# Attention scores with all 128 rows of TensorE in every matmul

## The chip, the cores and the metric

The kernel runs on one core of a Trainium2 chip. A core has a matrix engine (TensorE, in the profile PE, its weight loads PEld), a vector engine (VectorE, DVE), a scalar engine (ScalarE, ACT), a general engine (GpSimd, POOL) and DMA queues (SP and others). The metric is the device time of one execution in microseconds, as the median of three runs; lower is better.

## What is computed

The reference is a decoder trunk of two layers on 512 positions of width 1024, in float32. Layer 0 mixes tokens by windowed attention with sinks (8 query heads, 2 key heads of 64) beside a convolution module; layer 1 by dilated attention (8 heads of 64) beside a gated unit. A SwiGLU feed-forward part follows each mixer. The scores are what this case is about:

```python
s = jnp.einsum('bnqhgd,bnjhd->bnhgqj', qb, kk, preferred_element_type=jnp.float32) * (hd ** -0.5)
s = jnp.where(valid[None, :, None, None], s, -jnp.inf)
p = jnp.exp(s - m[..., None])
o = jnp.einsum('bnhgqj,bnjhd->bnqhgd', p.astype(v.dtype), vv, preferred_element_type=jnp.float32)
```

A head is 64 wide, so a score matmul has a contraction of 64 where TensorE has 128 rows.

## The kernel before

Nearly all products are made of float32 values split into a high part, which the matmul type `F32R` holds, and a low part, the rest. A weight product takes three matmuls: high with high, high with low, low with high (`acc3`, L200 to L202). Activations lie transposed: 128 channels on the partitions, 512 positions in the columns.

The order of PE's instructions is the program's own: `seq` is a clock in estimated time by which the weight products (`gemm0`, `gemm1`, `tok_gemm`) are interleaved with the steps of attention, which are generators that yield a cost and a waiting time. The constants of `C0` say how long after a query projection its scores come, and how long after the scores the values. The queues of the other engines are ordered by a planner when the kernel is built, from a model of its own; work marked `LATER` (the convolution taps, L470 to L478) fills their gaps.

In both mixers two heads share a tile: head b=0 in partitions 0 to 63, head b=1 in 64 to 127. Since a head needs only 64 rows, high and low parts are stacked on the two halves, so that one matmul of 128 rows gives two of the products, and a second matmul on 64 rows adds the third.

Layer 0 (`scores0`, L561). The queries of a head are stacked: `qss[b]` holds the high part in the rows of the head and the low part in the other half (L707, L708). `khh[b]` holds the high part of the keys in both halves (L687, L688), and `kl` the low part of both key heads, each in its own half (L689). For a block of 128 queries n = 1 to 3, a matmul on 128 rows (L582) gives high·high plus low·high, and one on 64 rows (L583) adds high·low, both with 256 keys in the columns. For block n=0 one float32 matmul on 64 rows with 128 keys takes the unsplit `qT` and `kT` (L580); the hardware makes it in two passes, which the profile counts as two matmuls. A step of `scores0` has two blocks of queries and both heads: n = 0 and 1 in eight instructions, then, after more of the projections, n = 2 and 3 in eight. Scores stand in PSUM banks 2 (b=0) and 3 (b=1). DVE reads them (L590, row minimum and mask), ACT takes the exponentials (L602), PE transposes the result (L406), ACT copies it (L409), PE multiplies with the values (L420), DVE normalises (L429), PE transposes back (L434). There are four such rounds, one for each query tile i.

Layer 1 (`stack`, L1085, and `scores1`, L1104). `qs` holds the high part of a head's queries in both halves, `ks` the high part of its keys in the head's half and the low part in the other (L1092 to L1096), `ql` the low part of the queries of both heads. Block n has (n+1)·128 keys: a matmul on 128 rows (L1118) and one on 64 rows (L1119) for each head, four instructions a step and four steps in a round, in four rounds. DVE reads with L1122, ACT takes exponentials with L1126.

Of the kernel before, what the change touches and what calls it, by code (L numbers as in the profile page):

```python
# [23 lines left out]
P = 128  # L24
# [109 lines left out]
def trunk_kernel(ctx: ExitStack, tc: tile.TileContext, xT, ws, cols, sinks, sgu_g, sgu_b,  # L134
# [308 lines left out]
    with ExitStack() as mx:  # L443
# [94 lines left out]
                free.extend((0, 1))  # L538
            return gemm0(free.pop(0))

        kT = mp.tile([P, S], F32, name="kT")


        khh = [mp.tile([P, S], F32R, name=f"khh{b}") for b in range(2)]
        kl = mp.tile([P, S], F32R, name="kl")
        rows = (slice(0, 64), slice(64, 128))
        Vt = mp.tile([P, NQ, P], F32, name="Vt")

        def v_tok(vT):
# [11 lines left out]
        def scores0(i):  # L561
            yield 0.0, C0["q"]
            while i >= 2 and ("V", i - 2) not in done:
                yield 0.0, 0.3
            qT, qss = qTs[i]
            Pm = mp.tile([P, 8, 2 * P], F32, name="Pm", bufs=2)
            nm = scr.tile([P, 8], F32, name="nm")
            l = scr.tile([P, 8], F32, name="l")
            for n2 in range(2):
                sb = [bank(2), bank(3)]  # L570
                for n1 in range(2):
                    n = 2 * n2 + n1
                    for b in range(2):
                        r = slice(64 * b, 64 * b + 64)
                        lo = max(n - 1, 0) * P
                        w = (n + 1) * P - lo
                        out = sb[b][:, n1 * 256 + 256 - w:n1 * 256 + 256]
                        q = slice(n * P, (n + 1) * P)
                        if n == 0:
                            T.matmul(out, qT[r, q], kT[r, lo:lo + w], start=True, stop=True)  # L580
                        else:
                            T.matmul(out, qss[b][:, q], khh[b][:, lo:lo + w], start=True, stop=False)  # L582
                            T.matmul(out, qss[b][r, q], kl[r, lo:lo + w], start=False, stop=True)  # L583
                for n1 in range(2):
                    n = 2 * n2 + n1
                    for b in range(2):
                        u = 2 * n + b
                        c0 = P if n == 0 else 0
                        hd = i + 4 * b
                        V.tensor_tensor_reduce(  # L590
                            out=Pm[:, u, c0:], in0=sb[b][:, n1 * 256 + c0:n1 * 256 + 256],
                            in1=mask0[:, c0:], scale=-0.125, scalar=nsink[:, hd:hd + 1],
                            op0=ALU.add, op1=ALU.min, accum_out=nm[:, u:u + 1])
                if n2 == 0:
                    yield 0.9, C0["S"]
            es = scr.tile([P, 8], F32, name="es")
            V.tensor_tensor(out=es.rearrange("p (n b) -> p n b", b=2),
                            in0=nm.rearrange("p (n b) -> p n b", b=2),
                            in1=sinkb[:, i:i + 5:4][:, None, :].to_broadcast([P, NQ, 2]), op=ALU.add)
            for u in range(8):  # L600
                c0 = P if u < 2 else 0
                A.activation(Pm[:, u, c0:], Pm[:, u, c0:], AF.Exp, bias=nm[:, u:u + 1], scale=-1.0,  # L602
                             accum_out=l[:, u:u + 1])
            A.activation(es, es, AF.Exp)
            rl = scr.tile([P, 8], F32, name="rl")
            V.tensor_add(rl, l, es)
            V.reciprocal(rl, rl)
            del qTs[i]
            pend[i] = Pm, rl, seq.t + 0.9 + C0["ST"]
            yield 0.9, 0.0  # L610
# [62 lines left out]
        for step in C0["steps"].split():  # L673
# [7 lines left out]
            elif kind == "k":  # L681
                ps = gemm_in(step)

                def after(ps=ps):
                    rope(ps, kT, tabs, V if "k" in C0["rope_v"] else G)
                    for b in range(2):
                        A.activation(khh[b][rows[b]], kT[rows[b]], AF.Copy)  # L687
                        A.activation(khh[b][rows[1 - b]], kT[rows[b]], AF.Copy)  # L688
                        V.tensor_tensor(out=kl[rows[b]], in0=kT[rows[b]], in1=khh[b][rows[b]], op=ALU.subtract)  # L689
            elif kind == "v":  # L690
                ps = gemm_in(step)

# [349 lines left out]
    with ExitStack() as mx:  # L1042
# [37 lines left out]

        rows = (slice(0, 64), slice(64, 128))

        def stack(qT, kT):  # L1085
            ql = mp.tile([P, S], F32R, name="ql", bufs=2)
            out = []
            for b in range(2):
                r, o = rows[b], rows[1 - b]
# [1 line left out]
                qs = mp.tile([P, S], F32R, name="st", bufs=8)  # L1091
                A.activation(qs[r], qT[r], AF.Copy)  # L1092
                A.activation(qs[o], qT[r], AF.Copy)
                V.tensor_tensor(out=ql[r], in0=qT[r], in1=qs[r], op=ALU.subtract)
                A.activation(ks[r], kT[r], AF.Copy)
                V.tensor_tensor(out=ks[o], in0=kT[r], in1=ks[r], op=ALU.subtract)  # L1096
                out.append((qs, ks))
# [6 lines left out]
        def scores1(i, qk, ql):  # L1104
# [6 lines left out]
            for n in range(NQ):  # L1111
# [2 lines left out]
                sb = [bank(2), bank(3)]  # L1114
                for b in range(2):
                    qs, ks = qk[b]
                    r = rows[b]
                    T.matmul(sb[b][:, :w], qs[:, q], ks[:, :w], start=True, stop=False)  # L1118
                    T.matmul(sb[b][:, :w], ql[r, q], ks[r, :w], start=False, stop=True)  # L1119
                for b in range(2):  # L1120
                    u = 2 * n + b
                    V.tensor_tensor_reduce(  # L1122
# [32 lines left out]
        for i in range(4):  # L1155
# [3 lines left out]
            ps = gemm1(1)  # L1159
            kT = mp.tile([P, S], F32, name="kT")  # L1160
            rope(ps, kT, tabs)
            seq.add("S1", scores1(i, *stack(qT, kT)))
            seq.add("V1", values1(i))


# [149 lines left out]
```

## Time and profile before

| | us |
|---|---|
| median of three runs | 1143.85 |
| lowest and highest | 1141.49, 1144.53 |
| the profiled execution, its own time | 1142.52 |
| its span, first to last instruction | 1140.8 |
| PE busy | 1093.2 (96%) |
| DVE busy | 704.1 (62%) |
| ACT busy | 568.5 (50%) |
| POOL busy | 244.4 (21%) |
| mean granted clock of TensorE | 0.98 |

A profile records each instruction's start and duration on its engine and what ended the wait ahead of it. Matmuls are pipelined: the duration of one overlaps the next, so what a matmul costs PE is the distance from its start to the next one's start. The operands `64*128` and `128*128` are the rows and columns of the array that a matmul uses; `64x256` is the operand that streams, 256 columns on 64 rows.

### The profile page before, as it was taken

What the parts mean: (1) busy time and instruction counts of PE and PEld (TensorE: products, weight loads), DVE (VectorE), ACT (ScalarE), POOL (GpSimd) and SP (SyncE); (2) the same over time, 40 slices, a digit from 0 to 9 for tenths busy, and PEclk for the clock granted to TensorE, in tenths of its full rate; (3) what the DMA queues carried; (4) which work ended last, traced back from release to release, by engine and by line L of the source; (5) the groups of instructions that cost most, each with busy time, mean ns of one, the idle gap of its engine ahead of it and who ended that gap; (6) DMA issues with size and microseconds to landing.
All of it is one profiled execution on the core that took longest, in us unless ns stands there. A gap on an engine that the chain in (4) does not pass through costs nothing.

```text
span 1140.8 us, 13569 instructions
## 1 busy us (share of the span) xinstructions
PE 1093.2 (96%) x5052; PEld 890.2 (78%) x5052; DVE 704.1 (62%) x1060; ACT 568.5 (50%) x920; POOL 244.4 (21%) x218
## 2 busy tenths in 40 slices
PE   6989899899999999999999999999899999999997
PEld 4867678788888888888887878787688888888785
DVE  6789875677565655664647545664865656556533
ACT  4477656664435343543546654445644353434533
POOL 5788655201101010100024200002011010101002
PEclk9989899899999999999999999999999999999999
DMA  5221102887867677621522111238878776776121
GB/s 212 74 75 48 46 19 92 214 227 190 181 185 148 184 142 208 139 47 56 167 92 67 45 38 42 88 97 219 218 188 182 185 148 185 142 209 138 29 74 74
DMA packets 42802, 145.87 MB, mean 128 GB/s; under 512 B 4848, under 2 KB 5744, under 8 KB 42736
## 3 DMA queue, kind: packets, MB, share of 16 engines
q1 hardware_dynamic: 31216, 103.06, 26.9%
q0 software_dynamic: 11520, 41.95, 21.7%
q8 instruction: 39, 0.64, 0.2%
q14 instruction: 27, 0.22, 0.1%
HBM read 142.89 MB, written 2.10 MB: 127 GB/s over the span
## 4 chain that ended last, share of the span: by engine, by line
PE 80%; DVE 7%; ACT 4%; issue 3%; POOL 3%; DMA 2%; SPq 0%; POOLq 0%; ACTq 0%; DVEq 0%
PE bank L200 11%; PE bank L892 11%; PE bank L895 11%; PE bank L894 11%; PE bank L201 10%; PE bank L202 10%; PE bank L261 2%; PE bank L420 2%; PE bank L263 2%; PE bank L262 2%; DMA raw<-in_ws 2%; PE bank L907 1%; PE bank L406 1%; DVE w2l L150 1%; PE bank L1119 1%
## 5 line engine op out<-in xcount | busy, mean ns | idle before, releaser
L150 DVE TENSOR_TENSOR w2l<-raw,w2h 128x1024 fp32r<-128x1024 f32 x140 | 171.5, 1226 | 203.4 <-ACT w2h L868 203.0
L868 ACT ACTIVATE w2h<-raw 128x1024 fp32r<-128x1024 f32 x140 | 148.0, 1059 | 207.3 <-PE bank L895 159.8
L173 ACT ACTIVATE w_hi<-raw 128x512 fp32r<-128x512 f32 x204 | 128.1, 629 | 199.1 <-PE bank L201 146.2
L858 POOL DMA_DIRECT2D raw<-in_ws x80 | 69.4, 879 | 558.9 <-DVE w2l L150 226.2
L150 DVE TENSOR_TENSOR w_lo<-raw,w_hi 128x512 fp32r<-128x512 f32 x161 | 115.2, 716 | 64.1 <-ACT w_hi L173 64.1
L892 PE MATMUL bank<-w2h,s 128*128 128x512 f32 x320 | 126.1, 394 | 3.6 <-ACT s L811 1.9
L894 PE MATMUL bank<-w2l,s 128*128 128x512 f32 x320 | 125.5, 392 | 1.8 <-DVE w2l L150 1.8
L895 PE MATMUL bank<-w2h,s 128*128 128x512 f32 x320 | 125.5, 392 | 0.0
L200 PE MATMUL bank<-xh,w_hi 128*128 128x512 f32 x272 | 115.4, 424 | 9.9 <-ACT xh L312 9.9
L201 PE MATMUL bank<-xl,w_hi 128*128 128x512 f32 x272 | 112.0, 412 | 2.8 <-DVE xl L313 2.8
L202 PE MATMUL bank<-xh,w_lo 128*128 128x512 f32 x272 | 110.9, 408 | 0.0
L200 PE MATMUL bank<-hh,w_hi 128*128 128x512 f32 x256 | 99.9, 390 | 0.0
L201 PE MATMUL bank<-hl,w_hi 128*128 128x512 f32 x256 | 99.8, 390 | 0.0
L202 PE MATMUL bank<-hh,w_lo 128*128 128x512 f32 x256 | 99.8, 390 | 0.0
L892 PE MATMUL bank<-w2h,xh 128*128 128x512 f32 x240 | 94.5, 394 | 0.0
L895 PE MATMUL bank<-w2h,xl 128*128 128x512 f32 x240 | 93.6, 390 | 0.0
L894 PE MATMUL bank<-w2l,xh 128*128 128x512 f32 x240 | 93.5, 390 | 0.0
L892 PEld LDWEIGHTS bank<-w2h,s 128*128 128x128 f32 x320 | 60.5, 189 | 16.7 <-ACT s L811 2.3
L200 PEld LDWEIGHTS bank<-xh,w_hi 128*128 128x128 f32 x272 | 54.3, 200 | 23.4 <-ACT xh L312 10.8
L894 PEld LDWEIGHTS bank<-w2l,s 128*128 128x128 f32 x320 | 60.4, 189 | 14.4 <-DVE w2l L150 2.1
L150 POOL TENSOR_TENSOR w_lo<-raw,w_hi 128x512 fp32r<-128x512 f32 x43 | 59.9, 1395 | 50.4 <-ACT w_hi L173 45.0
L895 PEld LDWEIGHTS bank<-w2h,s 128*128 128x128 f32 x320 | 60.5, 189 | 13.1 <-DVE s L150 0.4
(234 smaller groups left out, 2067.6 us busy)
## 6 DMA issues: line engine op xcount, KB each, us to landing
raw<-in_ws SPq DMA_DIRECT2D x181, 512.0 KB, 4.1
raw<-in_ws POOLq DMA_DIRECT2D x80, 512.0 KB, 5.5
h<-in_xT SPq DMA_DIRECT2D x8, 256.0 KB, 6.5
out_y<-xh SPq DMA_DIRECT2D x4, 256.0 KB, 2.0
out_y<-xl SPq DMA_DIRECT2D x4, 256.0 KB, 2.3
raw<-in_ws SPq DMA_DIRECT2D x2, 256.0 KB, 4.1
ropeC<-in_rope_c SPq DMA_DIRECT2D x2, 256.0 KB, 4.1
ropeS<-in_rope_s SPq DMA_DIRECT2D x2, 256.0 KB, 4.6
```

Of the source, the lines that this page charges most:

```text
L150: eng.tensor_tensor(out=out, in0=a, in1=b, op=ALU.subtract)
L173: A.activation(hi, src, AF.Copy)
L200: T.matmul(ps, hi, xh, start=start, stop=False)
L201: T.matmul(ps, hi, xl, start=False, stop=False)
L202: T.matmul(ps, lo, xh, start=False, stop=stop)
L261: T.matmul(ps[t], xh[:, c], hi, start=(k == 0), stop=False)
L262: T.matmul(ps[t], xh[:, c], lo, start=False, stop=False)
L858: nc.gpsimd.dma_start(t, ws[base + 8 * (g - 1) + 2 * BLOCK_OF[more] + q], accum_op=ALU.add)
L868: A.activation(hi, src, AF.Copy)
L892: T.matmul(ps[t], xh[:, c], wh[:, w], start=(start and j == 0), stop=False, skip_group_check=True)
L894: T.matmul(ps[t], xh[:, c], wl[:, w], start=False, stop=False, skip_group_check=True)
L895: T.matmul(ps[t], xl[:, c], wh[:, w], start=False, stop=(j == 3), skip_group_check=True)
```

## The change

Low parts get tiles of their own for each head, whose other half is zero, and every score matmul then takes all 128 rows. In layer 0 `kl` becomes two tiles; the half that holds no low part is filled with zeros once, by ACT from zeroed padding (`cp[0]`). Block n=0 is computed from the split operands as the others are, so it has four F32R matmuls on 128 rows in place of two float32 ones on 64 (four passes). `kT` moves from a tile of its own into the scratch buffer `gb`. In layer 1 four tiles `qlow` (two rounds by two heads) take the place of the two `ql`, with one half zeroed once by ACT; four fills of 64x512. The number of score instructions, their columns and their order stay.

```diff
-        kl = mp.tile([P, S], F32R, name="kl")
+        kl = [mp.tile([P, S], F32R, name=f"kl{b}") for b in range(2)]
+        for b in range(2):
+            A.activation(kl[b][rows[1 - b]], cp[0][rows[1 - b], 0:1].to_broadcast([64, S]), AF.Copy)
...
-                        if n == 0:
-                            T.matmul(out, qT[r, q], kT[r, lo:lo + w], start=True, stop=True)
-                        else:
-                            T.matmul(out, qss[b][:, q], khh[b][:, lo:lo + w], start=True, stop=False)
-                            T.matmul(out, qss[b][r, q], kl[r, lo:lo + w], start=False, stop=True)
+                        T.matmul(out, qss[b][:, q], khh[b][:, lo:lo + w], start=True, stop=False)
+                        T.matmul(out, qss[b][:, q], kl[b][:, lo:lo + w], start=False, stop=True)
...
+                    kT = scr.tile([P, S], F32, name="gb")
...
-                        V.tensor_tensor(out=kl[rows[b]], in0=kT[rows[b]], in1=khh[b][rows[b]], op=ALU.subtract)
+                        V.tensor_tensor(out=kl[b][rows[b]], in0=kT[rows[b]], in1=khh[b][rows[b]], op=ALU.subtract)
...
+        qlow = [[mp.tile([P, S], F32R, name=f"ql{p}{b}") for b in range(2)] for p in range(2)]
+        for p in range(2):
+            for b in range(2):
+                A.activation(qlow[p][b][rows[1 - b]], mhalf[rows[1 - b], 0:1].to_broadcast([64, S]),
+                             AF.Copy, scale=0.0)
...
-                V.tensor_tensor(out=ql[r], in0=qT[r], in1=qs[r], op=ALU.subtract)
+                V.tensor_tensor(out=ql[b][r], in0=qT[r], in1=qs[r], op=ALU.subtract)
...
-                    T.matmul(sb[b][:, :w], ql[r, q], ks[r, :w], start=False, stop=True)
+                    T.matmul(sb[b][:, :w], ql[b][:, q], ks[:, :w], start=False, stop=True)
```

## Rows read from the trace of the kernel before

**Rows 1.** Page, parts 1 and 4: busy time of each engine; shares of the chain.

```profile
PE 1093.2 (96%) x5052; PEld 890.2 (78%) x5052; DVE 704.1 (62%) x1060; ACT 568.5 (50%) x920; POOL 244.4 (21%) x218
...
PE 80%; DVE 7%; ACT 4%; issue 3%; POOL 3%; DMA 2%; SPq 0%; POOLq 0%; ACTq 0%; DVEq 0%
```

**Rows 2.** Windows of both mixers: stretch, length, busy by engine, clock, DMA share, GB/s.

```profile
36.00:177.00 141.00, 129.68 (x617) 102.51 (x616) 118.50 (x230) 91.20 (x191) 106.20 (x80) 0.93 0.16 53
...
583.00:705.00 122.00, 118.24 (x612) 94.10 (x611) 67.03 (x149) 68.15 (x143) 24.80 (x17) 0.99 0.17 53
```

**Rows 3.** Timeline of PE, layer 0, blocks 2 and 3: start, length, instruction.

```profile
93.67 0.39 PE L202 MATMUL bank<-xh,w_lo 128*128 128x512 f32 x1
93.89 0.28 PE L582 MATMUL bank<-khh,qs 128*128 128x256 f32 x1
94.10 0.38 PE L583 MATMUL bank<-kl,qs 64*128 64x256 f32 x1
94.41 0.38 PE L582 MATMUL bank<-khh,qs 128*128 128x256 f32 x1
...
96.28 0.50 PE L200 MATMUL bank<-xh,w_hi 128*128 128x512 f32 x1
96.62 0.40 PE L201 MATMUL bank<-xl,w_hi 128*128 128x512 f32 x1
```

**Rows 4.** Timeline of PE, layer 0, blocks 0 and 1 of the second round.

```profile
87.95 0.40 PE L202 MATMUL bank<-xh,w_lo 128*128 128x512 f32 x1
88.28 0.49 PE L580 MATMUL bank<-kT,qT 64*128 64x128 f32 x4
...
89.95 0.66 PE L434 MATMUL bank<-ident,on 128*128 128x128 f32 x4
```

**Rows 5.** Timeline of PE, layer 1, steps 0, 2, 3: first matmul, one behind them.

```profile
624.22 0.31 PE L1118 MATMUL bank<-st 128*128 128x128 f32 x1
...
625.22 1.11 PE L420 MATMUL bank<-Vt,pts 128*128 128x64 f32 x8
...
633.71 0.34 PE L1118 MATMUL bank<-st 128*128 128x384 f32 x1
...
635.08 0.66 PE L434 MATMUL bank<-ident,on 128*128 128x128 f32 x4
...
637.65 0.40 PE L1118 MATMUL bank<-st 128*128 128x512 f32 x1
...
639.61 0.39 PE L201 MATMUL bank<-xl,w_hi 128*128 128x512 f32 x1
```

**Rows 6.** Timeline of PE, eight transposes in a row, merged into one line.

```profile
620.77 1.04 PE L406 MATMUL bank<-ident,Pm 128*128 128x128 f32 x8
```

**Rows 7.** Timeline of PE, end of the first step of layer 0.

```profile
71.06 0.58 PE L583 MATMUL bank<-kl,qs 64*128 64x256 f32 x1 [2.22 <-DVE kl L689]
71.57 0.80 PE L200 MATMUL bank<-xh,w_hi 128*128 128x512 f32 x1
```

**Rows 8.** Timeline of DVE, layer 0; in brackets its idle time and what ended it.

```profile
79.19 0.48 DVE L590 CUSTOM_DVE_ANT_0 Pm<-bank,mask,nsink 128x256 f32<-128x256 f32 x1 [0.98 <-PE bank L583]
...
101.40 0.69 DVE L389 TENSOR_TENSOR ra<-bank,ropeC 128x512 f32<-128x512 f32 x1 [1.19 <-PE bank L202]
...
129.91 0.48 DVE L590 CUSTOM_DVE_ANT_0 Pm<-bank,mask,nsink 128x256 f32<-128x256 f32 x1 [2.41 <-PE bank L583]
```

**Rows 9.** Windows, as rows 2, of three shorter stretches.

```profile
101.40:124.60 23.20, 19.79 (x103) 15.53 (x102) 22.98 (x40) 14.78 (x28) 19.58 (x14) 0.92 0.15 46
70.00:77.00 7.00, 5.94 (x15) 4.61 (x16) 5.27 (x13) 4.42 (x11) 7.00 (x6) 0.55 0.22 75
585.00:590.00 5.00, 5.00 (x23) 4.13 (x22) 2.63 (x5) 1.27 (x2) 2.36 (x2) 1.00 0.23 83
```

**Rows 10.** Single lines of code: count, duration in ns (least/median/most), first and last start.

```profile
L1093 ACT ACTIVATE st<-qT x8: 628/630/634, 591.3 to 656.0; 64x512 fp32r<-64x512 f32 x8
...
L478 DVE SCALAR_TENSOR_TENSOR bank<-cp,cc,bank x72: 699/754/757, 39.4 to 166.6; 128x512 f32<-128x512 f32 x72
```

More of the change, by code (lines that the diff above doesn't have):

```diff
@@ L539, in gemm_in @@
             return gemm0(free.pop(0))
-        kT = mp.tile([P, S], F32, name="kT")
         khh = [mp.tile([P, S], F32R, name=f"khh{b}") for b in range(2)]
-        kl = mp.tile([P, S], F32R, name="kl")
+        kl = [mp.tile([P, S], F32R, name=f"kl{b}") for b in range(2)]
         rows = (slice(0, 64), slice(64, 128))
+        for b in range(2):
+            A.activation(kl[b][rows[1 - b]], cp[0][rows[1 - b], 0:1].to_broadcast([64, S]), AF.Copy)
         Vt = mp.tile([P, NQ, P], F32, name="Vt")
@@ L564, in scores0 @@
                 yield 0.0, 0.3
-            qT, qss = qTs[i]
+            qss = qTs[i][1]
             Pm = mp.tile([P, 8, 2 * P], F32, name="Pm", bufs=2)
@@ L573, in scores0 @@
                     for b in range(2):
-                        r = slice(64 * b, 64 * b + 64)
                         lo = max(n - 1, 0) * P
@@ L1083, in trunk_kernel, with stack @@
         rows = (slice(0, 64), slice(64, 128))
-        def stack(qT, kT):
-            ql = mp.tile([P, S], F32R, name="ql", bufs=2)
+        qlow = [[mp.tile([P, S], F32R, name=f"ql{p}{b}") for b in range(2)] for p in range(2)]
[3 more added lines that the diff above has]
+                             AF.Copy, scale=0.0)
+        def stack(i, qT, kT):
+            ql = qlow[i % 2]
             out = []
@@ L1116, in scores1 @@
                     qs, ks = qk[b]
-                    r = rows[b]
                     T.matmul(sb[b][:, :w], qs[:, q], ks[:, :w], start=True, stop=False)
-                    T.matmul(sb[b][:, :w], ql[r, q], ks[r, :w], start=False, stop=True)
+                    T.matmul(sb[b][:, :w], ql[b][:, q], ks[:, :w], start=False, stop=True)
                 for b in range(2):
@@ L1161, in trunk_kernel @@
             rope(ps, kT, tabs)
-            seq.add("S1", scores1(i, *stack(qT, kT)))
+            seq.add("S1", scores1(i, *stack(i, qT, kT)))
             seq.add("V1", values1(i))
```

## The prediction

> **What bounds the kernel.** The page comes first: PE is busy 96% of the span, no other engine over 62%, and the chain that ended last lies on PE for 80% [rows 1]. So time taken out of PE's stream counts, unless another engine holds PE at that place. The windows of the two mixers say where that may be: in layer 1 (583 to 705 us) PE is busy 118.2 of 122.0 us, DVE and ACT little more than half; in layer 0 (36 to 177) PE is busy 129.7 of 141.0, DVE 118.5, POOL 106.2, and the clock is 0.93 [rows 2]. There part of a gain can end in a wait. The timeline of PE is read next, by distances between starts, and last the timeline of DVE, for the places where it waits for PE.
>
> **What a score matmul costs now.** In a plain run of weight products a matmul of 512 columns comes 0.22 us after the one before (93.67 to 93.89). In a score step a matmul of half as many columns takes longer: the first, on 128 rows, is followed after 0.21, and from the second on every change between 64 and 128 rows comes 0.31 apart [rows 3]. Same engine, same type, fewer columns: what differs is the number of rows from one instruction to the next. Transposes, all on 128 rows with 128 columns, follow one another at (1.04-0.27)/7 = 0.11, where 0.27 is the length of one alone as the last of the eight [rows 6].
>
> **What it will cost.** No row has 128-row matmuls of 256 columns in a row. Two rows bound it: 0.11 (128 columns) below and 0.22 to 0.23 (512) above. The plain run gives 0.227/512 = 0.44 ns a column, so 256 columns stream in 0.114; that is nearest to the transposes' 0.11, so I take 0.12. By the same rate 384 columns take 0.17, 512 take 0.227, and 128 the 0.11 of the transposes. Both bounds stay for the range.
>
> **Layer 0, the sum on PE.** Blocks 2 and 3: from 93.89 to the second matmul behind the step, 96.62, is 2.73; less 0.23 for that L200 itself, 2.50. Eight matmuls at 0.12 make 0.96. Saved 1.54, four times: 6.2. Blocks 0 and 1: 87.95 to 89.95 is 2.00, less 0.23 for L202, 1.77 [rows 4]. Block 0 changes from four passes of float32 to four matmuls of 128 columns, 4 x 0.11, and block 1 takes 4 x 0.12: 0.92. Saved 0.85, three times: 2.5. The fourth of these steps, the first of the kernel, loses: today block 0 and most of block 1 are through when the last low part of the keys comes at 71.06, and one matmul is left, with L200 0.51 behind [rows 7]. After the change block 0 needs that low part as well, so the second head's low product and four matmuls of block 1 queue behind the wait: five, in a stretch where the clock is low [rows 9], so twice 0.11 to 0.12 each, about 1.1 in place of 0.51. I put down -0.5; the readers of these scores on DVE (L590) start later by about as much, and DVE has idle time behind them to take that up (5.27 of 7 us busy from 70 to 77) [rows 9]. Together 6.2+2.5-0.5 = 8.2.
>
> **How much of it arrives.** DVE's list is in order and nearly full here, so it can move forward only where it waits for PE today. Ahead of 101.4 these waits are 0.98, 0.16, 1.00 and 1.19; from 101.4 to 124.6 it works 22.98 of 23.20 us; behind that they are 1.43, 2.41, 0.97, 0.61 and 0.82 up to the last score step (three of the nine stand in [rows 8], the full stretch in [rows 9]). Walking down: L590 needs the first six of eight matmuls, so it comes 0.95 earlier, less the 0.5 lost, at 79; PE itself is held to that by the exponentials at 84, and by L429 at 90. At 101.4 PE has gained 2.6 and DVE, with 2.8 of waits and this gain at hand, also 2.6. The full stretch carries 2.6 through. Then the waits are long enough to follow PE: 5.0 at 135, 6.2 at 155. So 6.2 of 8.2 arrive; the rest ends in longer waits of PE for DVE and ACT. POOL has waits of its own before and behind the full stretch and is not tighter than DVE.
>
> **Layer 1.** Step 0: 624.22 to 625.22 is 1.00, becomes 4 x 0.11 = 0.44, saves 0.56. Step 1 is half of the eight matmuls of rows 3, 1.25 becoming 0.48: about 0.75. Step 2: 633.71 to 635.08 is 1.37, becomes 4 x 0.17 = 0.68: 0.69. Step 3: 637.65 to 639.61 less 0.23 is 1.73, becomes 4 x 0.227 = 0.91: 0.82 [rows 5]. One round 2.8, four rounds 11.3; the very first step waits for DVE between its two heads, so I count 0.4 there in place of 0.56: 11.1. PE has almost no waits here and DVE and ACT are half idle, so nearly all arrives: 11.0.
>
> **The small parts.** A zero fill costs as a copy of 64x512 does, 0.63 us on ACT [rows 10]. The four of layer 1 (2.5 us) come before the first rope, where ACT is busy 1.27 of 5 us [rows 9], the two of layer 0 (1.3 us) just behind the first weight products, and ACT is busy 91 of 141 us from there on [rows 2]: nothing on the path, and up to 1.3 and 2.5 us once if they land in front of a copy that PE awaits. `kT` in `gb` shares two buffers with the convolution gate; its life ends with the subtraction at 71, and nothing that I can place waits for it: zero, with one DVE wait of under 1 us as the upper end. The subtraction itself, its size and its number do not change. No DMA is added and none moved. What follows the mixers (norm sums, first weights of the feed-forward part) hangs on the mixers' end and moves with it.
>
> **The clock.** Three stretches in layer 0 as that of 70 to 77 run near the lower of the two levels (1.2 in place of 2.4 GHz; granted 0.55 in that window, after PE had waited 2.2 us at 71.06) [rows 7, 9]; each costs 7 x 0.45 = 3.2 us, and three of them make the 0.07 x 141 = 9.9 us that the window lacks [rows 2]. They follow waits of PE, and these waits stay or grow a little. I leave their number as it is, and count one stretch more or less, 3.2 us, into the range.
>
> **Sum.** 6.2 + 11.0 = 17.2. The profiled execution would go from 1142.5 to 1125.3; the median lies 1.3 above that execution, so 1143.85 - 17.2 = 1126.7, rounded to 1127.
>
> **Rivals.** (a) *The load lies open.* The first 128-row score matmul of a step, 256 columns, is followed after 0.21, which is 0.10 over its streaming [rows 3]; this could be a weight load that waits for the matmul before it, and might remain when all rows are alike. Then the steps cost columns plus 0.10: 0.15, 0.21, 0.26, 0.32. Layer 0 saves 4 x 0.82 + 3 x 0.33 - 0.7 = 3.6, of which 2.7 arrive, layer 1 0.40 x 4 + 0.41 x 4 + 0.33 x 4 + 0.45 x 4 = 6.4, with 0.2 off for the first step 6.2: 1135. Against it: transposes with all 128 rows and only 0.05 us of streaming follow at 0.11, and 512 columns at 0.22, not 0.32. The Trainium skill states a rule of this kind, in "TensorE: Matmul & The Clock Gate", Part 3 (Packing small matmuls — row/col tiling): a weight load overlaps a matmul in flight only when the two use different row groups. By that rule the change would take away the cover that 64 rows beside 128 might give, and rival (a) or worse would follow; rows 6 speak against it.
> (b) *DVE keeps all of layer 0.* If the planner's new order or the full stretch swallows what PE gains there, layer 1 alone is left: 1143.85 - 11 = 1133. For it: DVE 118.5 of 141 us; against it: nine waits for PE.
> (c) *Slower, by the order of the queues.* The planner builds the lists of DVE, ACT and POOL anew, from changed times and with six more ACT instructions. A convolution tap placed ahead of a score reader, L429 or a subtraction puts 0.75 us into PE's way [rows 10]. From 17.2/0.75 = 23 such taps of the 72 on, the gain is gone; with 30, 1149. For it: PE already waits for these lists; against it: the taps have the lowest priority.
> (d) *The change does not do what it says.* If the 0.31 came from two products of different operands into one bank and not from the rows, nothing is saved: 1143 to 1145. Against it: L200 to L202 change both operands at every matmul and follow at 0.22.
>
> **How the numbers follow.** My forecast has 0.68, (a) 0.12, (b) 0.10, (c) 0.05, (d) 0.05. The forecast's own range is 1120 to 1133: downward with all of layer 0's 8.2 arriving (2.0), one low-clock stretch less (3.2) and the runs' own spread (1.5); upward with one stretch more and a fill in PE's way (3.2 and 2.5). To hold eight in ten it must reach to (b) and (a), with the spread above (a): 1120 to 1137. A measurement of this kernel can tell a change of about 0.3%, 3.4 us, from none. Faster by more: the forecast, (a) and (b), less 0.02 for small parts gone wrong, 0.88. Within: (d) and a part of (c), 0.06. Slower: 0.06.
>
> **What would show it.** Right: score matmuls of 256 columns 0.11 to 0.13 apart, of 512 at 0.22 to 0.23; steps of blocks 2 and 3 near 1.0 us; the weight product behind a step no longer later than in a plain run; DVE's waits for PE of rows 8 gone or shrunk, PE's waits for DVE's L429 still there; in layer 0 about 6 us, in layer 1 about 11 us less from first to last score step. Wrong: 0.2 between score matmuls (rival a); steps short and the mixers as long as before (b); taps ahead of score readers (c). The prediction fails most easily if a low-clock stretch comes or goes, or where the lists of DVE in layer 0 are laid anew.

## The result, and the profile after

The kernel after takes 1123.7 us (median of four runs, 1120.3 to 1124.0) against 1142.7 of the kernel before in the same comparison: a ratio of 0.9836, 95% interval 0.9806 to 0.9866. Two further comparisons of the same two kernels gave 0.9885 (0.9848 to 0.9922; 1125.3 against 1137.9) and 0.9881 (0.9861 to 0.9902; 1124.35 against 1136.5). The gain is thus 12 to 19 us; 17 had been forecast, and 1127 us with a range from 1120 to 1137. The profiled execution took 1123.48 us, with a span of 1121.8. One execution of e2_layer1, a kernel told of below, took 2158.8 us, nearly twice as long as its others, and is left out of its median.

The page's busy times and the shares of the chain, as in [rows 1]:

```profile
PE 1073.6 (96%) x5052; PEld 888.4 (79%) x5052; DVE 701.2 (63%) x1060; ACT 571.7 (51%) x926; POOL 244.7 (22%) x218
...
PE 77%; DVE 8%; ACT 4%; issue 4%; POOL 4%; DMA 2%; POOLq 0%; SPq 0%; ACTq 0%; DVEq 0%
```

PE has as many instructions as before and is busy 19.6 us less; no other engine's busy time changed by more than 3.2 us. PE's share of the chain fell from 80% to 77%; DVE, POOL and issue took up one point each: a first hint that a part of the gain ended in waits.

The timeline of PE, a step of blocks 2 and 3 in layer 0 (start, length, instruction), the counterpart of [rows 3]:

```profile
89.53 0.39 PE L202 MATMUL bank<-xh,w_lo 128*128 128x512 f32 x1
89.75 0.28 PE L580 MATMUL bank<-khh,qs 128*128 128x256 f32 x1
89.87 0.28 PE L581 MATMUL bank<-kl,qs 128*128 128x256 f32 x1
...
90.58 0.28 PE L581 MATMUL bank<-kl,qs 128*128 128x256 f32 x1
90.70 0.40 PE L200 MATMUL bank<-xh,w_hi 128*128 128x512 f32 x1
90.93 0.39 PE L201 MATMUL bank<-xl,w_hi 128*128 128x512 f32 x1
```

Starts are 0.12 us apart where they were 0.31, from the first score matmul on. The weight product behind the step comes 0.12 after the last score, and its next one 0.23 later, as in any plain run. In layer 1, step 3 (512 columns), the starts are 0.22 to 0.23 apart; in step 0 (128 columns), 0.11 to 0.14 [rows 5]:

```profile
613.30 0.31 PE L1122 MATMUL bank<-st 128*128 128x128 f32 x1
613.44 0.27 PE L1123 MATMUL bank<-st,ql 128*128 128x128 f32 x1
613.56 0.27 PE L1122 MATMUL bank<-st 128*128 128x128 f32 x1
...
625.49 0.39 PE L1122 MATMUL bank<-st 128*128 128x512 f32 x1
625.72 0.39 PE L1123 MATMUL bank<-st,ql 128*128 128x512 f32 x1
...
626.40 0.39 PE L200 MATMUL bank<-xh,w_hi 128*128 128x512 f32 x1
```

Windows over the same instructions of PE in both kernels (columns as in [rows 2]): layer 0 from the last weight products before the first score to the last score step, and layer 1 from behind its first step to its end. First the kernel before, in windows that were not shown yet, then the kernel after:

```profile
62.33:163.42 101.09, 89.87 (x436) 69.92 (x434) 83.92 (x179) 68.39 (x157) 72.92 (x55) 0.90 0.13 42
606.48:692.72 86.24, 84.72 (x444) 65.95 (x443) 46.09 (x111) 49.01 (x112) 14.36 (x10) 1.00 0.15 50
```

```profile
59.24:154.43 95.19, 82.36 (x436) 70.12 (x434) 87.41 (x185) 68.68 (x157) 73.61 (x55) 0.87 0.14 45
597.83:673.90 76.07, 73.99 (x444) 64.47 (x443) 44.38 (x111) 48.30 (x112) 14.84 (x10) 1.00 0.17 56
```

To see where the difference of these lengths sits I split PE's time in three, instruction by instruction. The distance to the next start, less the wait in the next one's brackets, is the time PE spent on its own; where the granted clock was at the lower level (0.50, 1.2 in place of 2.4 GHz), half of that is put down as lost to the clock. The same split is used for all runs below. Layer 1 is counted here from shortly before its first score step.

| us | length | waits | lost to the clock | PE's own |
|---|---|---|---|---|
| layer 0, before | 101.1 | 11.2 | 9.5 | 80.4 |
| layer 0, after | 95.2 | 12.8 | 10.8 | 71.6 |
| layer 0, after, third profile (e6_after_third, below) | 96.2 | 14.9 | 9.2 | 72.0 |
| layer 1, before | 112.2 | 3.4 | 1.7 | 107.2 |
| layer 1, after | 101.9 | 4.1 | 1.7 | 96.1 |

PE's own time falls by 8.8 and 11.1 us. Layer 1 keeps 10.3 of it, layer 0 only 5.9. Of the 2.9 us that layer 0 does not keep, 1.6 are longer waits and 1.3 the clock's; in the third profile longer waits take 3.7 of 8.4. Beside these 16.2 us stand 3.1 us that went before any score was taken: there the profile before has a stretch at the lower clock (0.51 from 25 to 32 us), and the profile after has none. Between the mixers the kernel after loses 0.5. Together 18.8 of the 19.0 us by which the two spans differ.

### The profile page after: what moved, and what is told of

It is laid out like the page before. It is cut to its first block, busy times and chain, and to the rows that moved or that the text cites. A ratio compares the mean times of both kernels' runs of the same rounds, so it can differ in the third digit from the quotient of the medians.

```text
span 1121.8 us, 13570 instructions
## 1 busy us (share of the span) xinstructions
PE 1073.6 (96%) x5052; PEld 888.4 (79%) x5052; DVE 701.2 (63%) x1060; ACT 571.7 (51%) x926; POOL 244.7 (22%) x218
## 4 chain that ended last, share of the span: by engine, by line
PE 77%; DVE 8%; ACT 4%; issue 4%; POOL 4%; DMA 2%; POOLq 0%; SPq 0%; ACTq 0%; DVEq 0%
PE bank L894 11%; PE bank L891 11%; PE bank L893 11%; PE bank L200 10%; PE bank L201 10%; PE bank L202 10%; PE bank L261 2%; PE bank L263 2%; PE bank L262 2%; PE bank L420 2%; POOL yc L474 1%; DMA raw<-in_ws 1%; PE bank L906 1%; PE bank L406 1%; DVE w2l L150 1%
## 5 line engine op out<-in xcount | busy, mean ns | idle before, releaser
L173 ACT ACTIVATE w_hi<-raw 128x512 fp32r<-128x512 f32 x204 | 128.1, 629 | 185.3 <-PE bank L201 138.8
L200 PE MATMUL bank<-xh,w_hi 128*128 128x512 f32 x272 | 113.6, 418 | 10.8 <-ACT xh L312 10.8
L201 PE MATMUL bank<-xl,w_hi 128*128 128x512 f32 x272 | 110.8, 407 | 1.9 <-DVE xl L313 1.9
L202 PE MATMUL bank<-xh,w_lo 128*128 128x512 f32 x272 | 110.2, 405 | 0.0
L200 PE MATMUL bank<-hh,w_hi 128*128 128x512 f32 x256 | 99.8, 390 | 0.0
L202 PE MATMUL bank<-hh,w_lo 128*128 128x512 f32 x256 | 99.6, 389 | 0.0
L201 PE MATMUL bank<-hl,w_hi 128*128 128x512 f32 x256 | 99.6, 389 | 0.0
L891 PEld LDWEIGHTS bank<-w2h,s 128*128 128x128 f32 x320 | 60.4, 189 | 14.9 <-ACT ga L957 1.9
L200 PEld LDWEIGHTS bank<-xh,w_hi 128*128 128x128 f32 x272 | 54.1, 199 | 22.4 <-ACT xh L312 11.7
```

Source lines behind the costliest of these rows:

```text
L173: A.activation(hi, src, AF.Copy)
L200: T.matmul(ps, hi, xh, start=start, stop=False)
L201: T.matmul(ps, hi, xl, start=False, stop=False)
L202: T.matmul(ps, lo, xh, start=False, stop=stop)
L891: T.matmul(ps[t], xh[:, c], wh[:, w], start=(start and j == 0), stop=False, skip_group_check=True)
```

## The experiments

### Each layer alone

`e1_layer0` takes the new code of layer 0 with the old layer 1, `e2_layer1` the reverse. The lines by which they differ from the kernel before are the two parts of the diff ahead of the prediction; its core in e1_layer0 is

```diff
-                        if n == 0:
-                            T.matmul(out, qT[r, q], kT[r, lo:lo + w], start=True, stop=True)
-                        else:
-                            T.matmul(out, qss[b][:, q], khh[b][:, lo:lo + w], start=True, stop=False)
-                            T.matmul(out, qss[b][r, q], kl[r, lo:lo + w], start=False, stop=True)
+                        T.matmul(out, qss[b][:, q], khh[b][:, lo:lo + w], start=True, stop=False)
+                        T.matmul(out, qss[b][:, q], kl[b][:, lo:lo + w], start=False, stop=True)
```

and in e2_layer1

```diff
-                    T.matmul(sb[b][:, :w], ql[r, q], ks[r, :w], start=False, stop=True)
+                    T.matmul(sb[b][:, :w], ql[b][:, q], ks[:, :w], start=False, stop=True)
```

> Only layer 0 has the change; layer 1 is as before. My theory: about 6 us of the gain are layer 0's (5.9 between the first score step and the end of layer 0 in the two profiles), so about 1136.5 us against 1142.7. Rival, DVE keeps layer 0's gain: 1141 to 1143. A second question is the first 36 us, ahead of any score: before ran a stretch of them at the lower clock (from about 25 to 32 us) and the changed kernel did not, 3.1 us apart. If that is chance from one execution to the next, the stretch is there in some kernels and not in others, whichever change they have; if the two zero fills at the start of ACT's queue do it, it is gone here.

> Only layer 1 has the change; layer 0 is as before. Theory: 10 to 11 us, 1132 us against 1142.7, and together with the kernel that has only layer 0's part the sum of the whole change (19). Rival, the gain of one layer hangs on the other (by the phase of the clock or the planner's order): the two parts add up to 14 or less, or to 24 or more. The first 36 us have no zero fill here: if the fills remove the stretch at the lower clock, it is there; if it is chance, it may be either.

Measured: 1134.7 us for layer 0 alone, ratio 0.9966 (0.9949 to 0.9982), a gain of 3.9 us (2.0 to 5.8); 1127.7 for layer 1 alone, 0.9898 (0.9854 to 0.9942), a gain of 11.6 (6.6 to 16.6). The window of layer 0 in e1_layer0, then that of layer 1 in e2_layer1:

```profile
60.38:155.52 95.14, 82.32 (x435) 70.12 (x434) 87.41 (x185) 68.68 (x157) 73.64 (x55) 0.87 0.13 45
```

```profile
603.85:679.97 76.12, 74.02 (x443) 64.50 (x442) 44.38 (x111) 48.29 (x112) 14.84 (x10) 1.00 0.17 56
```

The part with the new code has the length of the kernel after within 0.1 us; the other part has that of the kernel before (86.27 and 101.09). So neither layer's window hangs on the change in the other, and the gains add up within their intervals: 0.0034 and 0.0102 make 0.0136, between the 0.0115 and the 0.0164 of the whole. By time, layer 0 alone brought less than the 6 us expected of it, though its window is 6 us shorter than the one in the profile of the kernel before.

### What the change of rows costs

`e3_grouped1` is the kernel before with the order of a layer 1 step altered: both matmuls of 128 rows first, then both of 64. The same matmuls, one change of rows down and up in a step in place of two.

```diff
                 for b in range(2):
                     qs, ks = qk[b]
-                    r = rows[b]
                     T.matmul(sb[b][:, :w], qs[:, q], ks[:, :w], start=True, stop=False)
+                for b in range(2):
+                    ks = qk[b][1]
+                    r = rows[b]
                     T.matmul(sb[b][:, :w], ql[r, q], ks[r, :w], start=False, stop=True)
```

> The kernel before, with layer 1's scores reordered and nothing else: both heads' matmuls on 128 rows first, then both on 64 rows. The same instructions, half the changes of row count (two in a step in place of four). Theory, the cost sits in the change from one row count to the other: a step of 512 columns takes 1.2 us or less in place of 1.73, layer 1 gains 6 to 9 us, 1134 to 1137 us; the two 64-row matmuls lie on different halves of the array and may run side by side, which would save up to 0.2 us a step more. Rival, a matmul on 64 rows is slow in itself, wherever it stands: steps as before, 1142 to 1144 us.

`e9_one64` comes from the other side: the kernel after, with the last of the four matmuls of a layer 1 step put back on 64 rows.

```diff
-                    T.matmul(sb[b][:, :w], ql[b][:, q], ks[:, :w], start=False, stop=True)
+                    r = rows[b] if b else slice(0, P)
+                    T.matmul(sb[b][:, :w], ql[b][r, q], ks[r, :w], start=False, stop=True)
```

> The kernel after with one of the four score matmuls of each layer 1 step put back on 64 rows (the second head's low product, the last of the four); its columns and all other work stay. Theory (a price for each change of row count): the pair 128 to 64 comes about 0.2 us later than two of 128 rows, and the change back to 128 rows behind it costs up to 0.2 us again, seen on whatever matmul follows. Sixteen steps: layer 1's score region grows by 3 to 6 us. Rival (64 rows slow in themselves, in proportion to columns): the matmul on 64 rows takes twice its streaming, so 0.05 more at 128 columns and 0.23 at 512, and nothing is lost behind it: 2.3 us over sixteen steps, growing with the columns. Rival (nothing below two changes a step): no growth.

Measured: e3_grouped1 1130.25 us, ratio 0.9939 (0.9916 to 0.9962); e9_one64 1122.65 in a single run. Its total does not decide, since that execution lost less to the clock in layer 0 (5.6 us by the split above, against 10.8). Layer 1 does. The timeline of PE in e9_one64, steps 1 and 3:

```profile
593.10 0.28 PE L1124 MATMUL bank<-st,ql 128*128 128x256 f32 x1
593.22 0.28 PE L1122 MATMUL bank<-st 128*128 128x256 f32 x1
593.42 0.38 PE L1124 MATMUL bank<-st,ql 64*128 64x256 f32 x1
593.74 0.50 PE L200 MATMUL bank<-xh,w_hi 128*128 128x512 f32 x1
594.08 0.40 PE L201 MATMUL bank<-xl,w_hi 128*128 128x512 f32 x1
...
600.93 0.39 PE L1122 MATMUL bank<-st 128*128 128x512 f32 x1
601.25 0.49 PE L1124 MATMUL bank<-st,ql 64*128 64x512 f32 x1
601.67 0.50 PE L200 MATMUL bank<-xh,w_hi 128*128 128x512 f32 x1
602.01 0.39 PE L201 MATMUL bank<-xl,w_hi 128*128 128x512 f32 x1
```

Step 1: the distances are 0.20, 0.32 and 0.34 where all-128-row work has 0.12, 0.12 and 0.23; the excess is 0.08, 0.20 and 0.11. Step 3: 0.32, 0.42 and 0.34 against 0.23 each; 0.09, 0.19 and 0.11. Both make 0.39 us, with twice the columns in the second; in a step of 128 columns (from 609.35 us) the excess is 0.29. So the price belongs to the change of rows and does not grow in proportion to the columns, and it falls on the matmul of fewer rows, on the first of more, and on the one behind that. "64 rows are slow in themselves" falls: it wanted an excess that grows with the columns and nothing behind the step.

The account closes within 1 us. PE's own time in layer 1 is 96.1 in the kernel after and 102.0 in e9_one64: 5.9 us for 16 changes down and up, 0.37 each. Two for each step, as before had, would give 96.1 + 32 x 0.37 = 107.9; before has 107.2. And e3_grouped1 has one a step, like e9_one64, but 99.5. Its timeline says why it is 2.5 lower still:

```profile
615.23 0.61 PE L1117 MATMUL bank<-st 128*128 128x512 f32 x2
615.78 0.50 PE L1121 MATMUL bank<-st,ql 64*128 64x512 f32 x2
616.21 0.50 PE L200 MATMUL bank<-xh,w_hi 128*128 128x512 f32 x1
```

Two matmuls of 64 rows, one in each half of the rows, take 0.43 together up to the next start, and the single one of e9_one64 took 0.42. The second came at no cost that can be seen; by the trace it starts 3 ns behind the first. In the four sizes the matmul that it saves is worth 0.11 + 0.12 + 0.18 + 0.23, four times 0.64, 2.6 us. Grouping alone thus regained 7.4 of the 10.2 us of layer 1's window (86.2 to 78.8), without a single new tile.

### The stretch at the start

`e5_after_again` is the kernel after, with no line altered, beside the runs of each layer alone and of e3_grouped1.

> The changed kernel once more, unchanged, for the spread of its profile: 1123 to 1125 us. If the stretch at the lower clock from 25 to 32 us is chance, it can be there this time, and the score steps of 256 columns stay 0.12 apart; then some 3 us of the 19 in the two profiles are not the change's. If it is the change's, it is gone again.

Measured: 1125.3 us, the second comparison told above. Windows of the early weight products: first in this profile of the kernel after, then in its first profile.

```profile
26.50:30.00 3.50, 3.50 (x12) 2.85 (x11) 0.00 (x0) 0.00 (x0) 1.28 (x2) 0.52 0.33 103
```

```profile
7.40:31.10 23.70, 20.67 (x81) 15.34 (x82) 18.22 (x20) 12.48 (x21) 12.89 (x11) 1.00 0.58 213
```

The same kernel shows a low clock here in one execution and none in the other. Other kernels have such a stretch whichever change they contain: e1_layer0, with layer 0's zero fills, is at 0.50 from 25.2 to 28.6 us, e2_layer1, without them, from 26.1 to 29.5. The 3.1 us at the start of the profiled pair are therefore not put down to the change, nor to the zero fills, which run at 2.3 us in both profiles of the kernel after.

### Scores later, to close PE's waits

The profile after has 4.2 us of waits in the very first score step (the brackets: idle time, and what ended it), and a low clock behind it:

```profile
63.48 0.33 PE L580 MATMUL bank<-khh,qs 128*128 128x128 f32 x1 [0.67 <-ACT khh L687]
65.07 0.47 PE L581 MATMUL bank<-kl,qs 128*128 128x128 f32 x1 [1.26 <-DVE kl L688]
...
67.98 0.47 PE L581 MATMUL bank<-kl,qs 128*128 128x128 f32 x1 [2.23 <-DVE kl L688]
```

`e7_later0` puts this step later in PE's order:

```diff
-            yield 0.0, C0["q"]
+            yield 0.0, C0["q"] + (4.5 if i == 0 else 0.0)
```

`e8_later` does so in layer 1 as well, with

```diff
-            yield 0.0, C0["q1"]
+            yield 0.0, C0["q1"] + (2.2 if i == 0 else 0.0)
```

and `e6_after_third` is the kernel after, with no line altered, beside them.

> The kernel after, unchanged, beside the two kernels of this call that start the first scores later. It is the yardstick for them. Expected: 1120 to 1128 us; the wait for the keys' parts in the first score step of layer 0 (0.7, 1.3 and 2.2 us on three matmuls) is there again, since it comes from the order of the work; the number of low-clock stretches in layer 0 may differ by one (1.7 us for each 3.4 us of such a stretch), since it differed between two profiles of this same kernel.

> The kernel after, with the first round's first score step of layer 0 placed 4.5 us later in PE's order (by the constant in front of the generator), so that weight products fill the time in which PE waits for khh and kl (4.2 us of waits in the profile after). Theory: the wait is lost time on the path, and the low-clock stretch right behind it (65 to 72 us, 3.4 us lost) follows from it. Then 4 us less, and up to 7 if the low-clock stretch goes as well: 1116 to 1120. Rival: the readers on DVE start later and the wait turns up again at the exponentials or at the normalised output one step on; then 1122 to 1125. Second rival: the stretch of low clock comes elsewhere in layer 0; then the wait's 4 us alone.

> As the kernel before this in the list, and in layer 1 the first round's first score step is placed 2.2 us later too, where PE waits 2.0 us for the second head's stacked keys. Theory: 1 to 2 us less than that kernel, because layer 1 has no other tight engine. Rival: no difference, the wait moves to the next step.

Measured: 1124.35 for the kernel after, 1126.3 for e7_later0 (ratio to before 0.9911, 0.9896 to 0.9925), 1130.8 for e8_later (0.9947, 0.9931 to 0.9963). Neither later start gained anything. PE's waits in layer 0's window of e7_later0, the two largest groups by what ended them (sum, count, longest):

```profile
PE bank L406 <- ACT yn L634: 8.4, 3, 6.7
PE bank L420 <- ACT pts L409: 5.8, 2, 4.5
```

The wait for `kl` is gone and 6.7 us stand one step on, before the transposes of the weights of attention. PE starts the last score matmul of the step at 69.42 us, but DVE reads the first scores (L588) only at 73.16. Its timeline:

```profile
68.74 2.34 DVE L478 SCALAR_TENSOR_TENSOR bank<-cp,cc,bank 128x512 f32<-128x512 f32 x3
...
73.16 0.35 DVE L588 CUSTOM_DVE_ANT_0 Pm<-bank,mask,nsink 128x128 f32<-128x128 f32 x1
```

Five taps and a gate product stand ahead of the readers in DVE's list; the exponentials, and L634 behind them, follow. Waits in layer 0 are 17.4 in all against 14.9 in e6_after_third, the clock's loss is 7.3 against 9.2, and the length 96.6 against 96.2. So the first rival was right in kind, though the time lies above its range; the second held as well, as a stretch at 0.50 stands behind the new wait (79.8 to 86.6 us). e8_later took 4.5 us more than e7_later0, where its rival had no difference: PE's waits in layer 1 are 7.8 us against 4.1, since the wait for the stacked keys went but the copies of L409 now hold PE for 6.1 us in five waits, where e6_after_third has 2.5 in four.

### What holds layer 0: DVE's load, or the order?

`e10_before_halftaps` and `e11_after_halftaps` leave every second of the later convolution taps out on DVE.

```diff
-                    else:
+                    elif t % 2:
                         V.scalar_tensor_tensor(acc, src, w, acc, op0=ALU.mult, op1=ALU.add)
```

> The kernel before with every second of the convolution's later taps on DVE (L478) left out; its time is not that of the full computation. It is one of a pair: the same is left out of the kernel after. Theory (DVE's nearly full list is why not all that PE saves in layer 0 arrives): with DVE relieved by about 36 taps of 0.75 us, 27 us, PE's waits for L429 and the exponentials shrink in both kernels, and the pair differs in layer 0's score region by 8 to 9 us instead of 6. Rival (DVE is not the reason; what is missing was never saved on PE): the pair differs by the same 6. Low-clock stretches are taken out, 1.7 us for each 3.4 us of them.

> The other half of the pair: the kernel after with every second of the convolution's later taps on DVE left out; its time is not that of the full computation. Theory: 8 to 9 us less than the other kernel of the pair in layer 0's score region, low-clock stretches taken out, and 10 to 11 in layer 1, where no tap runs. Rival: 6 us in layer 0 as with all taps.

Measured: 1146.0 us for the one (five runs from 1134.1 to 1146.7) and 1121.4 for the other. The spread goes with the clock: the profiled execution of e10_before_halftaps took 1146 us, with a mean clock of 0.973, and stood at 0.50 from 143.4 to 167 us; the runs of 1134 and 1135 had 0.986. Only the split is compared. Layer 0 of both, first the kernel before with half the taps, then the kernel after:

```profile
58.59:164.73 106.14, 95.42 (x436) 74.96 (x435) 67.67 (x155) 68.78 (x156) 73.47 (x56) 0.84 0.13 40
```

```profile
58.76:151.97 93.21, 79.84 (x436) 67.87 (x434) 71.93 (x155) 67.58 (x156) 74.61 (x56) 0.91 0.15 46
```

DVE is busy 71.9 in place of 87.4 us after, and 67.7 in place of 83.9 before. PE's waits are 13.3 (12.8 and 14.9 with all taps) and 10.7 (11.2). A fifth of DVE's work taken away left the sum of the waits about as it was, though single waits changed. With the clock's loss taken out the pair differs by 4.8 us in layer 0 and by 9.5 in layer 1; with all taps layer 0 differs by 7.2 in the first profile and by 4.6 in the third. So the theory (8 to 9) falls: DVE's load is not what keeps the rest of the gain. That taps always give way is not shown; in e7_later0 five of them stood ahead of the score readers.

What PE does wait for is seen in the kernel after around its longest wait behind the first step (2.40 us; it was 1.14 in the same place before). Timelines of PE, of DVE and of ACT there:

```profile
101.85 0.39 PE L202 MATMUL bank<-xh,w_lo 128*128 128x512 f32 x1
104.64 1.09 PE L406 MATMUL bank<-ident,Pm 128*128 128x128 f32 x8 [2.40 <-ACT yn L634]
```

```profile
95.69 0.69 DVE L389 TENSOR_TENSOR ra<-bank,ropeC 128x512 f32<-128x512 f32 x1 [0.24 <-PE bank L202]
...
100.46 1.05 DVE L392 TENSOR_TENSOR qT<-ra,rb 128x512 f32<-128x512 f32 x1
```

```profile
101.55 1.28 ACT L706 ACTIVATE qs<-qT 64x512 fp32r<-64x512 f32 x2 [2.12 <-DVE qT L392]
102.86 0.72 ACT L473 ACTIVATE prod<-cp,cc 128x512 f32<-128x512 f32 x1
103.49 0.61 ACT L173 ACTIVATE w_hi<-raw 128x512 fp32r<-128x512 f32 x1
104.01 0.58 ACT L634 ACTIVATE yn<-bank 128x512 f32<-128x512 f32 x1
```

PE's transposes wait for a bank that L634 empties. L634 stands in ACT's list behind L706, and L706 waits 2.1 us for the rope of the next queries, which DVE starts when PE has made them and works on for 5.8 us. It is a loop from PE through DVE and ACT back to PE, and a shorter score step takes nothing from it. The loop was there in the kernel before too (timelines of ACT and of PE):

```profile
107.16 1.28 ACT L707 ACTIVATE qs<-qT 64x512 fp32r<-64x512 f32 x2 [2.02 <-DVE qT L392]
108.47 0.60 ACT L636 ACTIVATE yn<-bank 128x512 f32<-128x512 f32 x1
```

```profile
109.12 1.09 PE L406 MATMUL bank<-ident,Pm 128*128 128x128 f32 x8 [1.14 <-ACT yn L636]
```

There L636 follows the copies of the queries at once. In the kernel after, ACT's list has a tap's product (L473) and a split of weights (L173) between them, 1.2 us; PE's wait grew by about as much. L633, the DVE instruction that L634 waits for, was through at 102.3, so the growth is put down to the order of ACT's list, as the planner laid it anew; no run changes that order alone.

With half the taps (e11_after_halftaps, timelines of ACT and PE) this place is much the same: DVE works 4.9 us on the rope, with one tap between its parts and not two, and PE's wait is 0.2 us shorter.

```profile
98.48 1.28 ACT L706 ACTIVATE qs<-qT 64x512 fp32r<-64x512 f32 x2 [2.34 <-DVE qT L392]
```

```profile
101.57 1.09 PE L406 MATMUL bank<-ident,Pm 128*128 128x128 f32 x8 [2.17 <-ACT yn L634]
```

`e12_q_on_dve` takes L706 out of ACT's list and gives it to DVE; `e13_qk_on_dve` moves one of the two copies of each key head, too.

```diff
-                        A.activation(qss[b][rows[b]], qT[rows[b]], AF.Copy)
+                        V.tensor_copy(qss[b][rows[b]], qT[rows[b]])
```

and, in e13_qk_on_dve alone,

```diff
-                        A.activation(khh[b][rows[1 - b]], kT[rows[b]], AF.Copy)
+                        V.tensor_copy(khh[b][rows[1 - b]], kT[rows[b]])
```

> The kernel after with the high parts of the queries of layer 0 (L706, two copies of 64x512 a round) made on DVE in place of ACT. Theory (ACT's order holds PE, not DVE's fullness): in the profile after ACT stands idle 2.1 us at 101.55 and 1.0 us at 110.75 in front of L706 for DVE's rope, and the copies that PE waits for at 104.64 and, in another profile, at 114.79 (2.4 and 2.8 us) are queued behind it. With L706 gone from ACT's list these two waits of PE shrink to under 1 us, PE's waits in layer 0's score region fall from 12.8 to 15.0 us to about 10 to 11, and the time falls by 2 to 4 us: 1120 to 1123. Rival (DVE's list is the tight one): DVE gets 1.3 us a round more, and the waits of PE grow by about as much: 1126 to 1130.

> As the kernel before this in the list, and of the keys' high parts the copies into the other half (L687) are made on DVE too, so that ACT makes two copies in a row in place of four. Theory: the wait in the first score step of layer 0 (4.2 us on three matmuls in the profile after, for khh and kl) hangs on ACT's four copies of 0.65 us in a row and shrinks by 1 to 2 us; 1 to 2 us less than that kernel. Rival: DVE's own order decides (a rope and a tap stand ahead of the second subtraction there), and the wait stays or grows by the two copies: 0 to 2 us more.

Measured: 1129.7 us, ratio 0.9930 (0.9909 to 0.9951), and 1134.9, 0.9974 (0.9950 to 0.9998): some 5 and 10 us above the kernel after in its later comparisons. The new copies on DVE (count, least/median/most ns), the largest groups of PE's waits in layer 0, and L634 on ACT, in e12_q_on_dve:

```profile
L706 DVE CAST qs<-qT x8: 827/1386/1490, 47.4 to 118.5; 64x512 fp32r<-64x512 f32 x8
```

```profile
PE bank L434 <- DVE on L429: 8.4, 3, 4.5
PE bank L581 <- DVE kl L688: 4.2, 2, 2.9
```

```profile
107.13 0.60 ACT L634 ACTIVATE yn<-bank 128x512 f32<-128x512 f32 x1 [1.59 <-DVE bs L633]
```

The copy takes 1.39 us on DVE where ACT takes 0.63 [rows 10], and PE's waits grow from 12.8 to 22.4 us, mainly for L429. The wait before L406 shrinks only from 2.4 to 2.0: without L706 ahead of it, L634 waits 1.6 us for DVE's statistics (L633), which stand in DVE's list behind the same rope. So the rival held: work put into DVE's list on the way from the queries to the scores cost PE most of its length (8 copies, 11 us; 7.5 to 9.6 us more of waits), while taps taken out of that list gained nothing. In e13_qk_on_dve neither expectation held: the waits of the first score step stay (6.5 us against 6.7 in e12_q_on_dve), and the 5 us more stand at L429, 13.5 us of waits against 8.4. Which order of the lists would bring out the rest stays open; none of the complete kernels above beats the kernel after.

## Why the prediction was right, and where it was not

**What a score matmul costs.** Right to a hundredth inside a step: 0.12, 0.17 to 0.18, 0.22 to 0.23 and 0.11 for 256, 384, 512 and 128 columns. Behind transposes the second matmul is later, by 0.03 to 0.08: 0.14 at 128 columns (613.30 to 613.44) and 0.20 at 256 (617.01 to 617.21); and where 256 columns follow 128 the first distance is 0.17 (84.36 to 84.53). No rows change there, and why it is so is not shown. Rival (a) is out: the first score matmul of a step of blocks 2 and 3 is now followed after 0.12, so the 0.21 of [rows 3] belonged to the 64-row matmul behind it, as the 0.08 to 0.09 in e9_one64 say. Rival (d) is out too, since two products of different operands into one bank follow at 0.12; the argument given against it was not quite right, as L200 and L201 use the same high part of the weights. The rule in the Trainium skill, "TensorE: Matmul & The Clock Gate", Part 3, by which a weight load overlaps a matmul in flight only for different row groups, does not show here from 256 columns on: these matmuls all use all rows and follow one another at the rate of their columns. At 128 columns they come 0.11 apart, where that rate would give 0.06; what sets this floor is not shown.

**Layer 0 on PE.** Predicted 6.2 + 2.5 for seven steps; PE's own time over all eight fell by 8.8. The first step was put at -0.5: from the L202 ahead of it to the L200 behind it takes 6.80 us where it took 6.06, 0.74 longer, as the block that needs the low part queues behind the wait [rows 7]: the right mechanism, a quarter of a us too small.

**How much of it arrives.** 5.9 us of the forecast 6.2 in the profiled execution, 4.9 in the second and third profiles of the kernel after. The number was near; the reason given was wrong, so that it came so near is luck. I had DVE's full stretch from 101 to 125 limit the gain [rows 9], and with half of the later taps gone the sum of PE's waits stood. What I took for a bound by load is, at the longest wait behind the first step, a loop through three lists, made longer by the new order of ACT's. The DVE wait of 1.19 that starts it stood in [rows 8]; its other end, PE's wait for L636, I did not follow. The list of DVE's waits for PE also left out two of the longest, 4.09 us ahead of L429 at 147.05 and 2.12 at 77.51. DVE did move forward as predicted: its waits of 0.98, 1.19 and 2.41 in that group have gone, shrunk to 0.24 and gone, and it is busy 92% of layer 0's window, from 83%. PE's waits for L429 are still there, but fell from 3.1 to 1.6 us. Rival (b) is out, as e1_layer0 is faster than the kernel before; but its 3.9 us are less than the windows show.

**Layer 1.** Predicted 11.1 on PE, 11.0 arriving. PE's own time fell by 11.1, and 10.3 arrive, since waits grow by 0.7: for the second head's stacked keys at the start (2.0 us, 1.84 before) and once for a copy of L409 (0.56). Nothing hides in this layer, as said.

**The small parts.** The fills cost nothing: PE has no new wait near them, and they run at 2.3 us and at 549 us, both earlier than I had placed them. No wait for the shared buffer of `kT` shows. Rival (c), order, came in small: the 1.2 us that ACT's new list puts ahead of L634. e7_later0 shows it with taps ahead of score readers, as the rival had it.

**The clock.** "I leave their number as it is" did not hold for the profiled pair, as a stretch ahead of the scores was there before and not after: 3.1 us, about the 3.2 by which the range had been widened for it. It put the profiled execution 1.8 us below the 1125.3 of the sum, where the 16.2 us of the scores alone would have put it 1.0 above. Both errors lay inside the range. In the other comparisons, where the kernel before stood at 1136.5 to 1137.9 and not at 1142.7, the gain was 12.1 and 12.5. The forecast of 17.2 lies at the upper end of the second comparison's interval and above that of the third, so its nearness to the 19 of the first is in part luck. What of the 5 us there is the clock's is not settled: no profile of the kernel before was taken in them. The runs that list both show the link only roughly (1133.9 us at a mean clock of 0.987, 1144.4 at 0.978).

## What to carry to other kernels

Here a matmul that followed one with another number of rows paid for it, at 512 columns as at 256: before packing two products into one matmul and a half, compare distances between starts with those in a plain run, and either fill the rows with zeros or group the matmuls of equal rows. When PE's time shrinks on a path that loops through other engines, take PE's own time, its waits and the clock apart: own time was forecast to within a tenth here (8.2 and 11.1 us against 8.8 and 11.1), and waits took part of it back. To learn whether an engine's load is the cause of a wait, both take work from its list and add some; here only the second moved the sum of the waits. And when a wait grows, compare the order of the lists of the engine that ends it, before and after.

## What the runs showed of the hardware

- One change of rows down to 64 and up again cost 0.39 us in a step of 256 and in one of 512 columns: 0.08 to 0.09 at the 64-row matmul, 0.19 to 0.20 at the next, 0.11 at the one behind that (e9_one64). In a step of 128 columns it was 0.29.
- Two matmuls of 64 rows in the two halves of the rows, one right behind the other, took as long as one: 0.43 against 0.42 with 512 columns (e3_grouped1, e9_one64).
- The same kernel has stretches at the lower clock in one execution and not in another, over the same work: 1.00 in the first profile of the kernel after from 7 to 31 us, 0.52 from 26.5 to 30 in the second; and one of some 24 us at 0.50 in e10_before_halftaps.
- A copy of 64x512 into the matmul type took 1.39 us on DVE (median of eight, 0.83 to 1.49, e12_q_on_dve) and 0.63 on ACT [rows 10].
- F32R matmuls of 128 rows and 128 columns, each with its own weights, came 0.11 us apart, though one right behind a matmul of 512 columns was followed after 0.06 (83.96 to 84.02 us in the kernel after).
